# Down products of a two-FFN layer: weight sums on VectorE, and the last layer's outputs of tiles 0 to 3 in a sequence of their own

## The chip, the cores and the metric

The kernel runs on one core of a Trainium2 chip. The metric is the device time of one execution in microseconds (us). Five engines work side by side and meet at semaphores: TensorE (PE; PEld is its weight load), VectorE (DVE), ScalarE (ACT), GpSimd (POOL) and SyncE (SP, which here only issues DMAs). Each engine runs its own instructions strictly in the order in which the program wrote them, so an instruction that waits holds up all that stands behind it on its engine.

## The reference

One layer: a SwiGLU FFN, a token mixer (attention beside a state-space model), a second FFN, a final norm. 1024 tokens, width 1024, FFN width 2816, all float32. The change touches the third matrix product of each FFN, the sums behind it, and the final norm.

```python
def rms_norm(x, g):
    y = x * lax.rsqrt(jnp.mean(x * x, axis=-1, keepdims=True) + EPS)
    return y * g

def swiglu(h, w_gate, w_up, w_down):
    return (jax.nn.silu(h @ w_gate) * (h @ w_up)) @ w_down

x = x + 0.5 * swiglu(rms_norm(x, ffn1_norm), ffn1_w_gate, ffn1_w_up, ffn1_w_down)
...
x = x + 0.5 * swiglu(rms_norm(x, ffn2_norm), ffn2_w_gate, ffn2_w_up, ffn2_w_down)
return rms_norm(x, final_norm)
```

## The kernel before

Each large product is made in float32 precision from three matmuls (`mm3`, L179 to L181): both operands are split into a high part (`hi`, a cast on ACT, L86) and a rest (`lo`, a subtraction on DVE, L87), and the three matmuls are hi*hi, hi*lo and lo*hi. On top of that the product is cut into 2x2 blocks and done with seven block products in place of eight (Strassen's scheme in Winograd's form). This needs sums of blocks of both operands.

**The down product** (`down`, L671) multiplies the FFN's inner activations (in DRAM, `aD`) by `w_down`. `prod(m, ...)` is one of the seven products 0 to 6. It has 11 steps `c`; a step is four row tiles of 128 tokens times three matmuls of 128x512, so 12 matmuls. In the last `tail` steps the order is turned round: for each tile all those steps, then the tile is finished (`fin`).

**Operands.** `next_unit` hands out the operand pairs and makes those of two steps ahead (four units: `wp`, the weights, and `ap`, the activations, in turn). `down_units` (L628) lists them. For products 1 to 4 a unit `wp` has a `pre`: one sum of two weight blocks, 128x512, in place in the loaded weights `wraw` (`tt`, L640) or into a tile `T` (`t1_`, L645). There are 44 such sums in each down product, all on POOL. `pump` issues the `pre` of step c+1 before it makes `ap` of step c. The weights come in with products 0 and 1 (even blocks `ev`, odd blocks `od`); the sums of product 1 need `od`.

**Tiles.** The output is eight tiles of 128 tokens, each in two halves of 512 columns; `X[t]` first holds the residual, and `onto` (L682, DVE) adds a product's result to it. In product 4, `mix0` finishes half 0 of tiles 0 to 3, one tile in each of the first four steps: `onto` from the bank of an earlier product, `before` (the sum of squares on ACT, L204, whose result POOL scales, L206), and `onto` half 1 from a kept sum `U1`. `end0` then finishes half 1 as each tile's tail ends, and calls `after`. Product 5 loads the residual of tiles 4 to 7 (`x1`, step 0) and adds kept sums to them in the four steps from `late` on, which is 4. Product 6 ends tiles 4 to 7 (`end1`).

**The two callers.** In the first FFN `before` and `after` come from `normed`, in the second (and last) they are `gain_first` and `to_out`. `gain_first` also multiplies the half by the norm's gain (L1868, DVE). `to_out` takes the second half's squares, forms the reciprocal root of the mean (`rstd`, nine instructions of 128x1 from L212 to L217, on POOL for tiles 0 to 3 and on DVE for 4 to 7), and queues a function `g` that scales one half on ACT (L1877) and the other on DVE (L1878) and stores each by a DMA from SP (L1880) and from ACT (L1881). `settle(1)` runs the `g` of the tile before, so that it comes one tile late. `run` steps a main generator and its side generators in turn; in the last down product there is no side generator.

Of the kernel before, what the change touches and what calls it, by code (L numbers as in the profile page):

```python
# [18 lines left out]
D = 1024  # L19
# [3 lines left out]
NF = FF // 128  # L23
# [32 lines left out]
def tile_layer(ctx: ExitStack, tc: tile.TileContext, w, out: bass.AP, taps=None):  # L56
    nc = tc.nc
# [22 lines left out]
    def dt_(shape, name):  # L80
        return dram.tile(list(shape), F32, name=name)

    def split(hi, lo, src, scale=None, e=None):

        if scale is None:
            A.copy(out=hi, in_=src)  # L86
            (e or V).tensor_tensor(out=lo, in0=src, in1=hi.bitcast(F32), op=OP.subtract)  # L87
        else:
            A.activation(out=hi, in_=src, func=AF.Copy, scale=scale)
            V.scalar_tensor_tensor(lo, src, scale, hi.bitcast(F32), op0=OP.mult, op1=OP.subtract)  # L90
# [41 lines left out]
    def pair(name):  # L132

        t = slot(name, F32R)
        return t[:, :512], t[:, 512:]
# [47 lines left out]
    HALF = (slice(0, 512), slice(512, 1024))  # L183
# [8 lines left out]
    X, XN, SS = {}, {}, {}  # L192
# [15 lines left out]
    def rstd(t, E):  # L208


        y, r, m, p, z = (SS[t // 4][:, i, t % 4:t % 4 + 1] for i in range(5))
        E.tensor_scalar(y, y, 1.0 / D, p, op0=OP.mult, op1=OP.add)  # L212
        E.tensor_scalar(z, y, -0.5, None, op0=OP.mult)
        E.tensor_scalar(r.bitcast(I32), y.bitcast(I32), -0.5, float(0x5F3759DF), op0=OP.mult, op1=OP.add)
        for _ in range(3):
            E.tensor_scalar(m, r, r, z, op0=OP.mult, op1=OP.mult)
            E.tensor_scalar(r, m, 1.5, r, op0=OP.add, op1=OP.mult)  # L217

    def rstd_one(t, E):

        y, r, m, _, z = (SS[t // 4][:, i, t % 4:t % 4 + 1] for i in range(5))
        E.tensor_scalar(y, y, 1.0 / D, EPS, op0=OP.mult, op1=OP.add)
        E.tensor_scalar(z, y, -0.5, None, op0=OP.mult)
        E.tensor_scalar(r.bitcast(I32), y.bitcast(I32), -0.5, float(0x5F3759DF), op0=OP.mult, op1=OP.add)
        for _ in range(3):
            E.tensor_scalar(m, r, r, z, op0=OP.mult, op1=OP.mult)
            E.tensor_scalar(r, m, 1.5, r, op0=OP.add, op1=OP.mult)

    pend = []

    def settle(left=0):
        while len(pend) > left:
            pend.pop(0)()
# [394 lines left out]
    def down_units(d, n, left):  # L628


        ev, od, t1 = {}, {}, {}

        def load(x, c, r):
            def f():
                x[c] = slot("wraw")
                nc.sync.dma_start(out=x[c], in_=d[128 * r:128 * r + 128, :])
            return f

        def tt(o, a, b, op):
            return lambda: G.tensor_tensor(out=o(), in0=a(), in1=b(), op=op)  # L640

        def t1_(c):
            def f():
                t1[c] = half_slot("T1")
                G.tensor_tensor(out=t1[c], in0=od[c][:, HALF[1]], in1=ev[c][:, HALF[0]], op=OP.subtract)  # L645
            return f

        for m in range(7):
            for c in range(n):
                def e(i, c=c):  # L650
                    return lambda: ev[c][:, HALF[i]]

                def o(i, c=c):
                    return lambda: od[c][:, HALF[i]]

                if m < 2:
                    loads.append(load((ev, od)[m], c, 2 * c + m))
                pre = {1: tt(e(1), o(1), e(1), OP.subtract), 2: tt(e(0), e(1), e(0), OP.add), 3: t1_(c),
                       4: tt(e(0), o(0), e(0), OP.subtract)}.get(m)
                raw = (e(0), o(0), e(0), lambda c=c: t1.pop(c), lambda c=c: od.pop(c)[:, HALF[1]], e(1),  # L660
                       lambda c=c: ev.pop(c)[:, HALF[0]])[m]

                def make(raw=raw):
                    p = pair("wp")
                    split(p[0], p[1], raw())
                    return p

                makes.append((len(loads), pre, make, 9))
                left(m, c)

    def down(n, src, scale, before, after, flag=None, tail=4):  # L671

        U1, U2, U4 = [{} for _ in range(3)]
        pts, late = {}, min(4, n - 1)

        def load_x_(h):
            for t in range(4 * h, 4 * h + 4):
# [85 lines left out]
    def when(flag, gen):  # L763
        while not flag:
            yield
        yield from gen
# [936 lines left out]
    X1, X2 = dt_((8, 128, 1024), "X1"), dt_((8, 128, 1024), "X2")  # L1703

    def run(main, *side, often=()):


        side = list(side)
        for x in main:
            for s in list(side):  # L1710
                if (x != MID or s in often) and next(s, "end") == "end":
                    side.remove(s)
        return side
# [70 lines left out]
    pts = [bank(k) for k in range(KD - 1)]  # L1784
# [4 lines left out]

    squares(0, ALL, 0)  # L1790
    rstd_one(0, V)
    norm_to(0)
    turn_first(0)
    squares(1, ALL, 0)
    rstd_one(1, G)
    for t in (2, 3):
        squares(t, ALL, 0)
# [36 lines left out]
    half0 = []  # L1834
# [22 lines left out]
    half0 = []  # L1857
# [5 lines left out]
    fg = slot("fgain")  # L1863
    A.dma_start(out=fg, in_=w["final_norm"][None, :].to_broadcast([128, D]))

    def gain_first(t, hh):
        squares(t, HALF[hh], 3)
        V.tensor_tensor(out=X[t][:, HALF[hh]], in0=X[t][:, HALF[hh]], in1=fg[:, HALF[hh]], op=OP.mult)  # L1868

    def to_out(t, hh):  # L1870
        squares(t, HALF[hh], 0)
        h, i = divmod(t, 4)
        rstd(t, V if t > 3 else G)

        def g():
            r, o = SS[h][:, 1, i:i + 1], out[0, t * 128:(t + 1) * 128]
            A.activation(out=XN[t][:, HALF[1 - hh]], in_=X[t][:, HALF[1 - hh]], func=AF.Copy, scale=r)  # L1877
            V.scalar_tensor_tensor(XN[t][:, HALF[hh]], X[t][:, HALF[hh]], r, fg[:, HALF[hh]],  # L1878
                                   op0=OP.mult, op1=OP.mult)
            nc.sync.dma_start(out=o[:, HALF[hh]], in_=XN[t][:, HALF[hh]])  # L1880
            A.dma_start(out=o[:, HALF[1 - hh]], in_=XN[t][:, HALF[1 - hh]])  # L1881

        pend.append(g)
        settle(1 if t < 7 else 2)

    drain(run(down(NF // 2, tile_of(X2), 0.5, gain_first, to_out, tail=6)))
    settle()


# [26 lines left out]
```

## Time and profile before

| what | value |
|---|---|
| median of 3 runs | 2109.62 us (2107.64 to 2111.92) |
| the profiled execution | 2110.38 us, span on the core 2108.6 us |
| PE busy in the span | 96%, 9359 matmuls |
| DVE, ACT, POOL busy | 72%, 38%, 21% |
| down product of the first FFN | about 465 to 655 us of the span |
| down product of the second FFN | about 1874 to 2099 us |

The profile is of one execution; its span starts with the first instruction. Rows of the timeline give an instruction's start, its length and, in brackets, how long its engine had been idle before it and what ended that. Rows of the stretches give each engine's busy time and, after an x, the number of instructions that touch the stretch.

### The profile page before, as it was taken

Reading aid. Unit: us, or ns where it says so; the run is one execution under the profiler, and the core shown is the slowest. Engines: PE = TensorE matmul, PEld = TensorE weight load, DVE = VectorE, ACT = ScalarE, POOL = GpSimd, SP = SyncE. Lnnn points to the kernel's source line nnn. Section 1 sums busy time; section 2 is a strip of 40 time slices with the busy share of each in tenths; the row PEclk is TensorE's granted clock in tenths of the full one; section 3 lists DMA queues with packets and bytes.
Section 4 is the critical chain, followed back from the end, with each engine's and each line's share of the span. In section 5 each row is a group of like instructions: output and inputs, shape, how many; then the busy total and the mean of one; then the engine's idle time right before and its main releaser. Section 6 shows DMA issues by size and latency. Waiting matters only on the chain.

```text
span 2108.6 us, 26589 instructions
## 1 busy us (share of the span) xinstructions
PE 2020.0 (96%) x9359; PEld 1618.7 (77%) x9359; DVE 1514.7 (72%) x2684; ACT 802.0 (38%) x1529; POOL 449.1 (21%) x450
## 2 busy tenths in 40 slices
PE   7899999999999899999999999998999999999988
PEld 5687888887868777777777668787788888887866
DVE  7888888678867777877855544625876776769776
ACT  6423323325345422222244652444323233235353
POOL 0121121126441100000000324422121211217350
PEclk9999999999999999999999999999999999999999
DMA  4225324348424143333344556431332233356432
GB/s 160 87 89 169 102 84 132 95 133 321 143 80 157 60 143 98 105 113 107 101 146 140 177 166 205 156 120 51 100 124 92 85 125 100 101 221 228 145 120 80
DMA packets 179561, 272.06 MB, mean 129 GB/s; under 512 B 23576, under 2 KB 110436, under 8 KB 179428
## 3 DMA queue, kind: packets, MB, share of 16 engines
q1 hardware_dynamic: 169008, 264.54, 37.1%
q10 hardware_dynamic: 10308, 5.81, 1.0%
q8 instruction: 74, 1.21, 0.2%
q14 instruction: 59, 0.48, 0.1%
q0 software_dynamic: 112, 0.02, 0.1%
HBM read 191.50 MB, written 81.17 MB: 129 GB/s over the span
## 4 chain that ended last, share of the span: by engine, by line
PE 49%; DVE 10%; DMA 3%; issue 2%; POOL 1%; ACT 1%; SPq 0%; DVEq 0%; ACTq 0%; POOLq 0%
PE bank L179 15%; PE bank L181 14%; PE bank L180 14%; DVE wp L87 2%; PE bank L1239 1%; DMA wraw<-in_ffn_w_down_dram 1%; PE bank L1278 1%; PE bank L1176 1%; PE bank L1263 1%; DVE T L283 1%; DVE ap L87 1%; DVE s L478 1%; PE bank L1174 1%; DVE S L385 1%; DMA al<-Ad 0%
## 5 line engine op out<-in xcount | busy, mean ns | idle before, releaser
L179 PE MATMUL bank<-T,wp 128*128 128x512 f32 x1008 | 399.4, 396 | 8.0 <-DVE F L336 4.2
L181 PE MATMUL bank<-T,wp 128*128 128x512 f32 x1008 | 395.6, 392 | 9.2 <-DVE wp L87 9.2
L180 PE MATMUL bank<-T,wp 128*128 128x512 f32 x1008 | 394.7, 392 | 1.7 <-DVE T L283 1.7
L87 DVE TENSOR_TENSOR wp<-wraw,wp 128x512 fp32r<-128x512 f32 x400 | 326.3, 819 | 82.2 <-ACT wp L86 81.2
L86 ACT CAST wp<-wraw 128x512 fp32r<-128x512 f32 x400 | 244.4, 620 | 294.1 <-DVE wraw L385 162.6
L179 PE MATMUL bank<-b,wp 128*128 128x512 f32 x756 | 304.8, 403 | 17.0 <-DVE s L478 13.6
L181 PE MATMUL bank<-b,wp 128*128 128x512 f32 x756 | 298.8, 395 | 3.5 <-DVE wp L87 3.5
L181 PE MATMUL bank<-wp,ap 128*128 128x512 f32 x744 | 293.7, 395 | 7.4 <-DVE ap L87 6.5
L180 PE MATMUL bank<-b,wp 128*128 128x512 f32 x756 | 298.8, 395 | 0.6 <-DVE b L278 0.6
L180 PE MATMUL bank<-wp,ap 128*128 128x512 f32 x744 | 291.9, 392 | 5.3 <-DVE wp L87 5.3
L179 PE MATMUL bank<-wp,ap 128*128 128x512 f32 x744 | 292.1, 393 | 2.5 <-ACT ap L86 2.5
L181 PEld LDWEIGHTS bank<-T,wp 128*128 128x128 f32 x1008 | 190.3, 189 | 53.2 <-DVE wp L87 13.2
L179 PEld LDWEIGHTS bank<-T,wp 128*128 128x128 f32 x1008 | 190.3, 189 | 51.8 <-issue 10.4
L180 PEld LDWEIGHTS bank<-T,wp 128*128 128x128 f32 x1008 | 190.6, 189 | 41.1 <-DVE T L283 2.9
L87 DVE TENSOR_TENSOR wp<-S,wp 128x512 fp32r<-128x512 f32 x189 | 151.8, 803 | 75.1 <-ACT wp L86 74.6
L86 ACT CAST wp<-S 128x512 fp32r<-128x512 f32 x189 | 116.8, 618 | 223.9 <-DVE S L385 180.4
L599 POOL TENSOR_TENSOR S<-sg 128x512 f32<-128x512 f32 x22 | 33.5, 1523 | 733.2 <-DVE sg L585 449.1
L179 PEld LDWEIGHTS bank<-b,wp 128*128 128x128 f32 x756 | 144.4, 191 | 55.4 <-issue 11.4
L181 PEld LDWEIGHTS bank<-wp,ap 128*128 128x128 f32 x744 | 140.3, 189 | 44.8 <-DVE ap L87 16.3
L181 PEld LDWEIGHTS bank<-b,wp 128*128 128x128 f32 x756 | 144.3, 191 | 36.3 <-DVE wp L87 5.6
L180 PEld LDWEIGHTS bank<-wp,ap 128*128 128x128 f32 x744 | 140.4, 189 | 37.5 <-DVE wp L87 8.6
L180 PEld LDWEIGHTS bank<-b,wp 128*128 128x128 f32 x756 | 144.5, 191 | 29.8 <-DVE b L278 1.2
(247 smaller groups left out, 2820.9 us busy)
## 6 DMA issues: line engine op xcount, KB each, us to landing
araw<-aD SPq DMA_DIRECT2D x154, 256.0 KB
wraw<-in_ffn_w_gate_dram SPq DMA_DIRECT2D x44, 512.0 KB
wraw<-in_ffn_w_up_dram SPq DMA_DIRECT2D x44, 512.0 KB
aD<-sg SPq DMA_DIRECT2D x88, 256.0 KB
wraw<-in_ffn_w_down_dram SPq DMA_DIRECT2D x44, 512.0 KB
wraw<-in_w_in_dram SPq DMA_DIRECT2D x38, 512.0 KB
aD<-S SPq DMA_DIRECT2D x66, 256.0 KB
x<-in_x_dram SPq DMA_DIRECT2D x16, 512.0 KB
```

The costliest lines, as they stand in the source:

```text
L86: A.copy(out=hi, in_=src)
L87: (e or V).tensor_tensor(out=lo, in0=src, in1=hi.bitcast(F32), op=OP.subtract)
L179: P.matmul(pt, lhsT=lhs[0], rhs=rhs[0], start=start, stop=False, skip_group_check=more)
L180: P.matmul(pt, lhsT=lhs[0], rhs=rhs[1], start=False, stop=False, skip_group_check=more)
L181: P.matmul(pt, lhsT=lhs[1], rhs=rhs[0], start=False, stop=stop, skip_group_check=more)
L283: return lambda: V.tensor_tensor(out=p[1], in0=f, in1=p[0].bitcast(F32), op=OP.subtract)
L385: V.tensor_tensor(out=o, in0=c[a], in1=c[b], op=op)
L478: V.tensor_tensor(out=o, in0=pt, in1=t, op=OP.add)
L599: G.tensor_tensor(out=ab[o], in0=ab[a], in1=ab[b], op=op)
L1174: P.matmul(pt, lhsT=KT[:, 2 * q + g2, :], rhs=U[:, 2 * q + g2, :], start=True, stop=False)
L1176: P.matmul(pt[:, 1:128], lhsT=CAv[i][64 * g2:64 * g2 + 64, 128 * q:128 * q + 128], rhs=Vs[64 * g2:64 * g2 + 64, i, q, 0:127], start=False, ...
L1239: P.matmul(pts[j], lhsT=q[64 * j:64 * j + 64, 128 * b:128 * b + 128], rhs=k[64 * j:64 * j + 64, 128 * b + 128 - n:128 * b + 128], start=Tr ...
```

## The change

The sums of weights in the down products of both FFNs are issued on DVE in place of POOL, at the same places of the program. `late` becomes 6, in both FFNs. In the last down product, tiles 0 to 3 no longer take the gain in `gain_first` nor the root and the outputs in `to_out`; a side generator `out_first`, which starts when product 4 has ended, forms one root for the four tiles (`rstd_four`, 12 instructions of 128x4 on DVE) and then, one tile a step, both output halves on DVE with the gain (`gained`) and one DMA of the whole tile from SP. For tiles 4 to 7 `settle()` now runs the `g` of the tile before ahead of this tile's root, and the last tile's outputs are made and stored in quarters of 256 columns.

```diff
+    def rstd_four(h):
+        y, r, m, p, z = (SS[h][:, i] for i in range(5))
+        V.scalar_tensor_tensor(y, y, 1.0 / D, p, op0=OP.mult, op1=OP.add)
+        V.tensor_scalar(z, y, -0.5, None, op0=OP.mult)
+        V.tensor_scalar(r.bitcast(I32), y.bitcast(I32), -0.5, float(0x5F3759DF), op0=OP.mult, op1=OP.add)
+        for _ in range(3):
+            V.tensor_tensor(out=m, in0=r, in1=r, op=OP.mult)
+            V.tensor_tensor(out=m, in0=m, in1=z, op=OP.mult)
+            V.scalar_tensor_tensor(r, m, 1.5, r, op0=OP.add, op1=OP.mult)
...
-            return lambda: G.tensor_tensor(out=o(), in0=a(), in1=b(), op=op)
+            return lambda: V.tensor_tensor(out=o(), in0=a(), in1=b(), op=op)
...
-                G.tensor_tensor(out=t1[c], in0=od[c][:, HALF[1]], in1=ev[c][:, HALF[0]], op=OP.subtract)
+                V.tensor_tensor(out=t1[c], in0=od[c][:, HALF[1]], in1=ev[c][:, HALF[0]], op=OP.subtract)
...
-        pts, late = {}, min(4, n - 1)
+        pts, late = {}, min(6, n - 1)
...
     def gain_first(t, hh):
         squares(t, HALF[hh], 3)
-        V.tensor_tensor(out=X[t][:, HALF[hh]], in0=X[t][:, HALF[hh]], in1=fg[:, HALF[hh]], op=OP.mult)
+        if t > 3:
+            V.tensor_tensor(out=X[t][:, HALF[hh]], in0=X[t][:, HALF[hh]], in1=fg[:, HALF[hh]], op=OP.mult)
+    def gained(t, hh):
+        r = SS[t // 4][:, 1, t % 4:t % 4 + 1]
+        V.scalar_tensor_tensor(XN[t][:, HALF[hh]], X[t][:, HALF[hh]], r, fg[:, HALF[hh]], op0=OP.mult, op1=OP.mult)
+    def out_first():
+        yield
+        rstd_four(0)
+        for t in range(4):
+            yield
+            for hh in range(2):
+                gained(t, hh)
+            nc.sync.dma_start(out=out[0, t * 128:(t + 1) * 128], in_=XN[t])
+            del XN[t], X[t]
     def to_out(t, hh):
         squares(t, HALF[hh], 0)
-        h, i = divmod(t, 4)
-        rstd(t, V if t > 3 else G)
+        if t < 4:
+            return
+        settle()
+        rstd(t, V)
...
+            n, w_ = (2, 256) if t == 7 else (1, 512)
+            for j in range(n):
+                a, b = (slice(512 * x + w_ * j, 512 * x + w_ * j + w_) for x in (1 - hh, hh))
...
         pend.append(g)
-        settle(1 if t < 7 else 2)
+    half0 = []
+    drain(run(down(NF // 2, tile_of(X2), 0.5, gain_first, to_out, half0, tail=6), when(half0, out_first())))
```

Three places in the order of the instructions. First, VectorE at the start of product 4 of the second FFN, before (`wp` and `ap` are the rests of the operands, `x<-bank` and `x<-U` the two `onto`, `x<-x,fgain` the gain):

```order
L87 TENSOR_TENSOR wp<-wraw,wp 128x512
L87 TENSOR_TENSOR ap<-araw,ap 128x512
L682 SCALAR_TENSOR_TENSOR x<-bank_15170,x 128x512
L1868 TENSOR_TENSOR x<-x,fgain 128x512
L682 SCALAR_TENSOR_TENSOR x<-U,x 128x512
L87 TENSOR_TENSOR wp<-wraw,wp 128x512
L87 TENSOR_TENSOR ap<-araw,ap 128x512
```

and in the change:

```order
L87 TENSOR_TENSOR wp<-wraw,wp 128x512
L651 TENSOR_TENSOR wraw<-wraw 128x512
L87 TENSOR_TENSOR ap<-araw,ap 128x512
L693 SCALAR_TENSOR_TENSOR x<-bank_15170,x 128x512
L693 SCALAR_TENSOR_TENSOR x<-U,x 128x512
L87 TENSOR_TENSOR wp<-wraw,wp 128x512
L651 TENSOR_TENSOR wraw<-wraw 128x512
L87 TENSOR_TENSOR ap<-araw,ap 128x512
```

The weight sum stands between the two splits of each step, and the gain is gone. The second place is ScalarE at the end of product 4 of the second FFN, before (casts, squares `xn,ss<-x`, output halves and their DMAs):

```order
L86 CAST ap<-araw 128x512
L204 ACTIVATE xn,ss<-x 128x512 x2
L1877 ACTIVATE xn<-x,ss 128x512
L1881 DMA out_dram<-xn 128x512
L204 ACTIVATE xn,ss<-x 128x512
L1877 ACTIVATE xn<-x,ss 128x512
L1881 DMA out_dram<-xn 128x512
L204 ACTIVATE xn,ss<-x 128x512
L1877 ACTIVATE xn<-x,ss 128x512
L1881 DMA out_dram<-xn 128x512
L86 CAST wp<-wraw 128x512
```

and in the change:

```order
L86 CAST wp<-wraw 128x512
L86 CAST ap<-araw 128x512
L204 ACTIVATE xn,ss<-x 128x512 x4
L86 CAST wp<-wraw 128x512
L86 CAST ap<-araw 128x512
```

Nothing that needs the root stands any more between the squares and the next casts. The third place is VectorE from the end of product 4 to product 5 of the second FFN, before (`x<-bank` is `onto` for half 1 of tiles 2 and 3, `xn<-x,ss,fgain` an output half):

```order
L682 SCALAR_TENSOR_TENSOR x<-bank_15681,x 128x512
L1878 SCALAR_TENSOR_TENSOR xn<-x,ss,fgain 128x512
L682 SCALAR_TENSOR_TENSOR x<-bank_15685,x 128x512
L1878 SCALAR_TENSOR_TENSOR xn<-x,ss,fgain 128x512
L87 TENSOR_TENSOR wp<-wraw,wp 128x512
L87 TENSOR_TENSOR ap<-araw,ap 128x512
```

and in the change:

```order
L693 SCALAR_TENSOR_TENSOR x<-bank_15681,x 128x512
L693 SCALAR_TENSOR_TENSOR x<-bank_15685,x 128x512
L87 TENSOR_TENSOR wp<-wraw,wp 128x512
L87 TENSOR_TENSOR ap<-araw,ap 128x512
L87 TENSOR_TENSOR wp<-wraw,wp 128x512
L87 TENSOR_TENSOR ap<-araw,ap 128x512
L232 SCALAR_TENSOR_TENSOR ss<-ss 128x4
L233 TENSOR_SCALAR ss<-ss 128x4
L234 TENSOR_SCALAR ss<-ss 128x4
L236 TENSOR_TENSOR ss<-ss 128x4
L237 TENSOR_TENSOR ss<-ss 128x4
L238 SCALAR_TENSOR_TENSOR ss<-ss 128x4
```

The last three rows come twice more; then each of the next four steps has its two splits and one tile's two output halves (L1884), and the four steps after these the kept sums of tiles 4 to 7, which before stood two steps earlier.

## Rows read from the trace of the kernel before

**Rows 1.** The page, engines: busy us, share of the span, instructions.

```profile
PE 2020.0 (96%) x9359; PEld 1618.7 (77%) x9359; DVE 1514.7 (72%) x2684; ACT 802.0 (38%) x1529; POOL 449.1 (21%) x450
```

**Rows 2.** Stretches in us: length, busy us (x instructions) by engine, PEclk, DMA share, GB/s.

```profile
515.00:530.00 15.00, 13.54 (x56) 9.82 (x54) 15.00 (x10) 5.21 (x10) 14.05 (x9) 1.00 0.23 70
600.00:617.00 17.00, 14.19 (x51) 8.90 (x51) 16.21 (x19) 8.71 (x17) 7.70 (x6) 1.00 0.00 0
1925.00:1938.00 13.00, 11.63 (x48) 8.36 (x47) 13.00 (x9) 4.55 (x8) 12.32 (x8) 1.00 0.24 67
2006.00:2028.00 22.00, 17.25 (x60) 11.69 (x59) 20.42 (x24) 9.96 (x20) 10.81 (x8) 0.92 0.00 1
2039.00:2048.00 9.00, 6.51 (x21) 4.70 (x20) 6.31 (x11) 6.74 (x14) 7.85 (x13) 0.81 0.77 277
1950.00:1990.00 40.00, 40.00 (x178) 33.14 (x177) 32.70 (x36) 14.93 (x26) 17.81 (x11) 1.00 0.57 184
1888.00:1920.00 32.00, 32.00 (x143) 26.48 (x142) 26.52 (x25) 21.26 (x37) 19.48 (x13) 1.00 1.04 412
```

**Rows 3.** Line 640, weight sums on POOL: ns min/median/max, first and last start us.

```profile
L640 POOL TENSOR_TENSOR wraw<-wraw x66: 1287/1734/1803, 488.5 to 2020.4; 128x512 f32<-128x512 f32 x66
```

**Rows 4.** Groups by line on DVE: count, busy us, mean ns, idle before.

```profile
L385 DVE TENSOR_TENSOR S<-wraw,S 128x512 f32<-128x512 f32 x63 | 57.1, 907 | 0.0
L385 DVE TENSOR_TENSOR S<-wraw 128x512 f32<-128x512 f32 x63 | 43.0, 683 | 0.0
```

**Rows 5.** Timeline of DVE, first FFN, product 4: start, length, instruction, idle before.

```profile
589.59 0.69 DVE L682 SCALAR_TENSOR_TENSOR x<-bank,x 128x512 f32<-128x512 f32 x1
...
593.77 0.68 DVE L682 SCALAR_TENSOR_TENSOR x<-bank,x 128x512 f32<-128x512 f32 x1
594.37 0.68 DVE L682 SCALAR_TENSOR_TENSOR x<-U,x 128x512 f32<-128x512 f32 x1
595.80 1.66 DVE L87 TENSOR_TENSOR wp<-wraw,wp 128x512 fp32r<-128x512 f32 x1 [0.76 <-ACT wp L86]
...
602.20 0.68 DVE L682 SCALAR_TENSOR_TENSOR x<-bank,x 128x512 f32<-128x512 f32 x1
...
613.91 0.68 DVE L87 TENSOR_TENSOR ap<-araw,ap 128x512 fp32r<-128x512 f32 x1
```

**Rows 6.** Timeline of DVE, second FFN, product 4.

```profile
1998.20 0.69 DVE L682 SCALAR_TENSOR_TENSOR x<-bank,x 128x512 f32<-128x512 f32 x1
...
2004.72 0.69 DVE L1868 TENSOR_TENSOR x<-x,fgain 128x512 f32<-128x512 f32 x1 [0.79 <-ACT xn L204]
...
2013.20 0.68 DVE L682 SCALAR_TENSOR_TENSOR x<-bank,x 128x512 f32<-128x512 f32 x1
...
2025.64 0.68 DVE L87 TENSOR_TENSOR ap<-araw,ap 128x512 fp32r<-128x512 f32 x1
```

**Rows 7.** Timeline of ACT, second FFN, start of product 5.

```profile
2040.62 0.72 ACT L1877 ACTIVATE xn<-x,ss 128x512 f32<-128x512 f32 x1 [1.43 <-POOL ss L217]
...
2041.79 0.62 ACT L86 CAST wp<-wraw 128x512 fp32r<-128x512 f32 x1 [0.44 <-ACT xn L1877]
```

**Rows 8.** Timeline of PE: the first matmul after that wait, and the last one.

```profile
2042.98 0.50 PE L179 MATMUL bank<-wp,ap 128*128 128x512 f32 x1 [2.49 <-ACT ap L86]
...
2099.03 0.39 PE L181 MATMUL bank<-wp,ap 128*128 128x512 f32 x1
```

**Rows 9.** Timeline of POOL, second FFN: the first and the eleventh sum of product 1.

```profile
1897.02 1.29 POOL L640 TENSOR_TENSOR wraw<-wraw 128x512 f32<-128x512 f32 x1 [17.93 <-issue]
...
1915.96 20.11 POOL L640 TENSOR_TENSOR wraw<-wraw 128x512 f32<-128x512 f32 x12 [0.28 <-DMA wraw<-in_ffn_w_down_dram]
```

**Rows 10.** Timeline of DVE after the last matmul.

```profile
2100.01 0.68 DVE L682 SCALAR_TENSOR_TENSOR x<-bank,x 128x512 f32<-128x512 f32 x1
2101.56 0.21 DVE L212 TENSOR_SCALAR ss<-ss 128x1 f32<-128x1 f32 x1 [0.86 <-ACT xn L204]
...
2103.61 1.41 DVE L1878 SCALAR_TENSOR_TENSOR xn<-x,ss,fgain 128x512 f32<-128x512 f32 x2
```

**Rows 11.** Timeline of SP's DMA issues, the last two.

```profile
2104.38 0.99 SPq L1880 DMA_DIRECT2D out_dram<-xn  x2
```

More of the change, by code (lines that the diff above doesn't have):

```diff
@@ L1867, in gain_first @@
         squares(t, HALF[hh], 3)
-        V.tensor_tensor(out=X[t][:, HALF[hh]], in0=X[t][:, HALF[hh]], in1=fg[:, HALF[hh]], op=OP.mult)
+        if t > 3:
[12 more added lines that the diff above has]
+            del XN[t], X[t]
     def to_out(t, hh):
         squares(t, HALF[hh], 0)
-        h, i = divmod(t, 4)
-        rstd(t, V if t > 3 else G)
+        if t < 4:
+            return
+        settle()
+        rstd(t, V)
         def g():
[L1876 to L1881, printed above, removed]
+            h, i = divmod(t, 4)
+            o = out[0, t * 128:(t + 1) * 128]
+            n, w_ = (2, 256) if t == 7 else (1, 512)
+            for j in range(n):
+                a, b = (slice(512 * x + w_ * j, 512 * x + w_ * j + w_) for x in (1 - hh, hh))
+                r = SS[h][:, 1, i:i + 1]
+                A.activation(out=XN[t][:, a], in_=X[t][:, a], func=AF.Copy, scale=r)
+                V.scalar_tensor_tensor(XN[t][:, b], X[t][:, b], r, fg[:, b], op0=OP.mult, op1=OP.mult)
+                nc.sync.dma_start(out=o[:, b], in_=XN[t][:, b])
+                A.dma_start(out=o[:, a], in_=XN[t][:, a])
         pend.append(g)
-        settle(1 if t < 7 else 2)
-    drain(run(down(NF // 2, tile_of(X2), 0.5, gain_first, to_out, tail=6)))
+    half0 = []
+    drain(run(down(NF // 2, tile_of(X2), 0.5, gain_first, to_out, half0, tail=6), when(half0, out_first())))
     settle()
```

## The prediction
> **What bounds the kernel now.** I read the page's engine line first: PE is busy 96% of the span [rows 1], so only stretches in which PE stands still, and the end after its last matmul, can give time. Next the stretches. Where PE streams, 178 matmul records touch 40 us [rows 2]. A record is 0.39 us long [rows 8] and starts are 0.227 us apart, so 1.7 of the records only reach over an edge. For any stretch, time lost = length - (records - 1.7) x 0.2268. By this the two down products lose, in [rows 2]:
> - 515 to 530 (first FFN, product 1): 15 - 54.3 x 0.2268 = 2.7 us
> - 600 to 617 (first FFN, product 4): 17 - 49.3 x 0.2268 = 5.8 us
> - 1925 to 1938 (second FFN, product 1): 13 - 46.3 x 0.2268 = 2.5 us
> - 2006 to 2028 (second FFN, product 4): 22 - 58.3 x 0.2268 = 8.8 us
> - 2039 to 2048 (second FFN, product 5): 9 - 19.3 x 0.2268 = 4.6 us
>
> Together 24.4 us. The last two have a granted clock of 0.92 and 0.81 of 2.4 GHz, so a part of each ran at the lower level (1.2 GHz) after PE had stood; that part is in the lost time and goes with the standing.
>
> Then what PE waits for. In 515 to 530, DVE is busy for all 15.00 us with only 10 instructions [rows 2], 1.5 us each, while POOL is busy beside it. Free of POOL, two DVE instructions of this size start 0.60 us apart (593.77 and 594.37, [rows 5]); a split that runs while POOL sums takes 1.66 us (at 595.80, [rows 5]), and the sum takes POOL 1.73 where it takes 1.29 at best [rows 3]. So each slows the other. A step of PE is 12 matmuls, 2.72 us; two slowed splits take more than that, two free ones 1.2. In product 4 a second cause is added: the DVE is idle 0.76 us a step for ACT's cast [rows 5], because the cast stands on ACT behind the squares of the half that DVE has just finished, and in the second FFN 0.79 us more for the gain, which waits for the same squares [rows 6]. In product 5 of the second FFN the chain is another: ACT's output half waits for POOL's root, the casts stand behind it [rows 7], and PE waits 2.49 us for a cast [rows 8].
>
> **The change part by part.**
>
> *Weight sums to DVE.* 44 sums in each down product leave POOL. On DVE each adds one 128x512 instruction with two operands in SBUF. The nearest rows are the same operation on other weights: 0.68 us alone, 0.91 in the mean where POOL disturbs [rows 4]. In a row of such, start to start, it is 0.60 [rows 5]. I take 0.60, since POOL has no large work left there, and keep 0.90 for the range.
>
> Products 1 to 3: a step then costs DVE split, sum, split = 1.8 us against PE's 2.72. A loop limits it too: split 0.60, sum 0.68, ACT's cast of the next weights 0.62 [rows 7], together about 1.92. Both are under 2.72, so the losses of 515 to 530 and 1925 to 1938 go: **2.7 and 2.5 us**. If a sum cost 0.90 the loop would be 2.2, still under.
>
> Product 4: count from the first `onto` of a bank to the end of the rest of step 10's `ap`, which PE waits for. Before, first FFN: 589.59 to 613.91 + 0.68 = 25.0 us [rows 5]. Second FFN: 1998.20 to 2025.64 + 0.68 = 28.1 us [rows 6]. After: from `onto` to the next weight split stays 2.03 us (593.77 to 595.80, [rows 5]), since ACT's squares are still in the chain; then split, sum, split, 1.80, to the next `onto`: 3.83 a step, three steps 11.5. From the fourth `onto`: 2.03, four rounds of the loop at 1.92, then 0.60 + 0.68: 11.0. The first `onto` comes one sum later: 0.6. In all 23.1 us in both FFNs. So the first gains **1.9**, the second **5.0** us (it loses the gain and its wait as well). A step of 3.83 is still longer than 2.72: of the 5.8 and 8.8 us some 3.8 stay in each. With 0.90 a sum, eight sums are on that way, 2.4 us: the first FFN would lose 0.5, the second gain 2.6. If instead the squares dropped out of the chain, all 14.6 would go.
>
> *`late` = 6.* Eight `onto` move two steps later in product 5, to steps 6 to 9: there two splits and two `onto`, 2.4 us of a step of 2.72. It hides under PE; if it did not, 4 x 0.6 us are at stake.
>
> *Outputs of tiles 0 to 3.* The four roots leave POOL and ACT has only the squares there, so casts follow at once: the 2039 to 2048 loss goes, **4.6 us**. What is late next is DVE: `rstd_four` is 12 small instructions; nine of 128x1 take 2.05 us (2101.56 to 2103.61, [rows 10]), so I take 2.7, at most 3.5. It waits for the last squares, and behind it on DVE stand the splits of steps 4 and later of product 5. By my count from product 4's end: `onto` 0.9, squares 0.7, cast 0.6, four splits 2.4, root 3, splits of step 4 1.2: about 9 us, where PE wants them at 4 x 2.72 + 0.45 = 11.3. After that a step has two splits and two output halves, 0.6 x 2 + 0.7 x 2 = 2.6, just under 2.72. So it is hidden, with some 2 us in hand. On SP the four output DMAs wait for DVE, and loads of `araw` stand behind them; those are for at least six steps later (two that are made ahead and four that are loaded beyond them, `rb`), 16 us, so nobody waits. ACT is rid of four output halves.
>
> *The end.* The last matmul starts at 2099.03 [rows 8], its `onto` at 2100.01 [rows 10], about 0.55 us late, since DVE still did the former tile's root and output. With that output put into the 0.86 us wait for the squares [rows 10], DVE is in time: 0.55. Behind the last root two halves took 1.41 us [rows 10]; now two quarters, 0.4 each, and on ACT copy, issue, copy, issue, some 1.5: no gain. The last issue starts at 2105.04 (0.33 before the end of the two, [rows 11]), 3.5 us before the span's end, with 256 KB; now 128 KB; at the 412 GB/s of [rows 2] that is 0.3 less. Sum **0.9 us** (0 to 1.5). The Trainium skill (DMA: Bandwidth & Descriptors, Anatomy of one DMA) speaks against cutting a transfer up: each pays about 2.0 us whatever its size, and bytes at 436 GB/s on top. The 3.5 us behind the last 256 KB agree that most of it is not bytes; whether the fixed parts of two quarters on one queue run side by side, no row shows. If they came one after the other, this term would by the page be a loss of about 1 us, and the sum below 15.7.
>
> **The sum.** 2.7 + 1.9 + 2.5 + 5.0 + 4.6 + 0.9 = 17.6 us. The profiled execution took 2110.38; 2092.8. The median of the runs is 0.8 lower (2109.62): **2092.0 us**. The first FFN's 4.6 must pass through the mixer; PE is its bound too, so I let it pass.
>
> **The rivals.**
> - *DVE becomes the bound.* The sums cost 0.90, the root delays the splits, the end gains 0.3: 2.7 - 0.5 + 2.5 + 2.6 + 4.6 + 0.3 = 12.2, so 2097.4. For: DVE is at 72% [rows 1], and steps of product 4 stay over 2.72. Against: with POOL gone its own instructions get shorter.
> - *The waits of product 4 go altogether.* 24.4 + 1.2 = 25.6, so 2084.0. For: a chain of 3.83 a step for four steps can be covered if DVE starts ahead. Against: DVE waits for PE at the end of product 3 (`keep`), so it starts product 4 with two steps in hand and no more.
> - *The sums wait for the weights on DVE, slower than before.* POOL could wait for `od` with nobody behind it; on DVE the split of step c's `ap` stands behind the sum of step c+1. The blocks arrive 1.89 us apart (1897.02 to 1915.96, ten intervals, [rows 9]) with DMA at 412 GB/s [rows 2]. Product 1 starts 11 steps of 2.72 us after 1874, near 1903.9. Step 9's split is ready at 1897.0 + 10 p + 1.3, and wanted at 1903.9 + 9 x 2.72 + 0.45: at p = 1.89 it is 11 us early; from p = 3.05 PE waits. To eat 17.6 and 4 more in two FFNs, p must be 4.1, that is 190 GB/s. Then about 2114. Nothing new is loaded there.
> - *The gain does not come through.* What PE gains is lost again where a wait of another kind ends at the same time: within 0.2% of before, about 2108.
>
> **How the numbers follow.** My forecast (some waits of product 4 stay) 0.70, with 2088 to 2097 as its own range; DVE as the bound 0.13; all waits gone 0.09; slower 0.04; no gain 0.04. The range reaches from 2086 to 2098, so that it takes in the dear sums and half the way to the case with no waits. 0.2%, 4.2 us, is about what a measurement of this kernel can tell from no change. Faster by more than that 0.92, within it 0.04, slower 0.04.
>
> **What would show it.** In the profile after: weight sums on DVE near 0.68 us each, POOL empty in both down products but for the small instructions; no loss of PE in product 1 of either FFN; in product 4 of both a loss of 3 to 5 us with DVE idle some 0.8 us a step for ACT's cast, and both about equal; no loss of 2 us and more in product 5 of the second FFN; the last `onto` within 0.5 us of the last matmul's start. I am wrong in the main if product 1 still loses time (then POOL was not the cause), or if product 5 shows a new wait for DVE behind the root of four tiles.

## The result, and the profile after

The changed kernel takes **2090.84 us** (median of 4 runs, 2090.54 to 2092.66) against 2109.64 us for the kernel before (4 runs beside it): a ratio of 0.9916, with a 95% interval of 0.9902 to 0.993. That is 18.8 us faster, and the interval leaves out 1. The prediction was 2092.0 us, with a range of 2086 to 2098.

In the profiled execution the span is 2088.8 us. The engine line of the page (busy us, share of the span, instructions), which answers to [rows 1]:

```profile
PE 2012.4 (96%) x9359; PEld 1618.5 (77%) x9359; DVE 1484.3 (71%) x2785; ACT 799.7 (38%) x1526; POOL 290.4 (14%) x326
```

VectorE has 101 instructions more than before and is busy 30 us less. GpSimd has lost 159 us. PE has the same number of matmuls and is busy 7.6 us less. (A matmul that follows a wait is recorded as 0.50 us long, one in a stream as 0.39 [rows 8], so less waiting shortens this figure too.)

The weight sums on VectorE, which answer to [rows 3] (one line's instructions: ns min/median/max, first and last start):

```profile
L651 DVE TENSOR_TENSOR wraw<-wraw x66: 682/684/693, 488.4 to 2009.6; 128x512 f32<-128x512 f32 x66
```

Each of these 66 takes 0.68 to 0.69 us, where POOL took 1.29 to 1.80. The other 22 of the 88, on line 656, take the same. The stretches, which answer to [rows 2] (length, busy us and, after the x, instructions of PE, PEld, DVE, ACT, POOL; granted clock; DMA share; GB/s):

```profile
514.00:529.00 15.00, 15.00 (x67) 12.41 (x67) 13.87 (x23) 8.45 (x15) 0.00 (x0) 1.00 0.34 115
598.00:612.00 14.00, 12.49 (x49) 8.39 (x48) 13.24 (x23) 8.00 (x16) 0.19 (x1) 1.00 0.00 1
1917.00:1930.00 13.00, 13.00 (x59) 10.77 (x58) 11.41 (x19) 6.85 (x12) 0.00 (x0) 1.00 0.39 119
1999.00:2015.00 16.00, 14.51 (x58) 10.16 (x58) 14.59 (x25) 9.26 (x20) 0.39 (x2) 1.00 0.12 35
2030.00:2042.00 12.00, 12.00 (x55) 9.93 (x54) 12.00 (x20) 5.55 (x11) 0.00 (x0) 1.00 0.87 299
```

With the formula of the prediction, lost = length - (records - 1.7) x 0.2268, the terms read as follows:

| place | lost before | lost after | gained | forecast |
|---|---|---|---|---|
| first FFN, product 1 | 2.7 | 0.2 (no wait) | 2.5 | 2.7 |
| first FFN, product 4 | 5.8 | 14 - 47.3 x 0.2268 = 3.3 | 2.5 | 1.9 |
| second FFN, product 1 | 2.5 | 0 | 2.5 | 2.5 |
| second FFN, product 4 | 8.8 | 16 - 56.3 x 0.2268 = 3.2 | 5.6 | 5.0 |
| second FFN, product 5 | 4.6 | 0 | 4.6 | 4.6 |
| last matmul's start to the span's end | 9.54 | 8.51 | 1.03 | 0.9 |
| sum | | | 18.7 | 17.6 |

(For the last row the last matmuls start at 2099.03 and 2080.26, and the spans to the hundredth are 2108.56 and 2088.77 us; the differences are taken before rounding.) The loss of product 4 is the one that stays. VectorE there, in the first FFN, which answers to [rows 5] (start, length, instruction, and in brackets how long VectorE had been idle and what ended that):

```profile
593.46 0.69 DVE L87 TENSOR_TENSOR wp<-wraw,wp 128x512 fp32r<-128x512 f32 x1 [0.76 <-ACT wp L86]
594.07 0.68 DVE L651 TENSOR_TENSOR wraw<-wraw 128x512 f32<-128x512 f32 x1
594.67 0.69 DVE L87 TENSOR_TENSOR ap<-araw,ap 128x512 fp32r<-128x512 f32 x1
595.27 0.68 DVE L693 SCALAR_TENSOR_TENSOR x<-bank,x 128x512 f32<-128x512 f32 x1
595.87 0.68 DVE L693 SCALAR_TENSOR_TENSOR x<-U,x 128x512 f32<-128x512 f32 x1
597.32 0.69 DVE L87 TENSOR_TENSOR wp<-wraw,wp 128x512 fp32r<-128x512 f32 x1 [0.76 <-ACT wp L86]
...
602.99 0.69 DVE L87 TENSOR_TENSOR wp<-wraw,wp 128x512 fp32r<-128x512 f32 x1
603.59 0.69 DVE L651 TENSOR_TENSOR wraw<-wraw 128x512 f32<-128x512 f32 x1
604.19 0.69 DVE L87 TENSOR_TENSOR ap<-araw,ap 128x512 fp32r<-128x512 f32 x1
604.79 0.69 DVE L87 TENSOR_TENSOR wp<-wraw,wp 128x512 fp32r<-128x512 f32 x1
```

A step goes from 593.46 to 597.32, 3.86 us, while PE needs 2.72: four starts 0.60 apart, then the 0.69 of the last `onto` and 0.76 idle for ACT's cast. After the four steps with `onto` a step is 1.80 us without any idle time (602.99 to 604.79), and VectorE catches up.

At the end, VectorE after the last matmul (which starts at 2080.26), answering to [rows 10]:

```profile
2080.69 0.69 DVE L693 SCALAR_TENSOR_TENSOR x<-bank,x 128x512 f32<-128x512 f32 x1 [0.39 <-PE bank L181]
2081.30 0.74 DVE L1912 SCALAR_TENSOR_TENSOR xn<-x,ss,fgain 128x512 f32<-128x512 f32 x1
2082.24 0.21 DVE L212 TENSOR_SCALAR ss<-ss 128x1 f32<-128x1 f32 x1 [0.20 <-ACT xn L204]
...
2084.41 0.88 DVE L1912 SCALAR_TENSOR_TENSOR xn<-x,ss,fgain 128x256 f32<-128x256 f32 x2
```

Now VectorE is idle until PE has the bank: the last `onto` starts 0.43 us after the last matmul's start, where it was 0.98 before. The output of tile 6 (2081.30) fills the wait for ACT's squares.

### The profile page after: what moved, and what is told of

Its sections match the earlier page's. It is cut to its first block, busy times and chain, and to the rows that moved or that the text cites. A ratio compares the mean times of both kernels' runs of the same rounds, so it can differ in the third digit from the quotient of the medians.

```text
span 2088.8 us, 26458 instructions
## 1 busy us (share of the span) xinstructions
PE 2012.4 (96%) x9359; PEld 1618.5 (77%) x9359; DVE 1484.3 (71%) x2785; ACT 799.7 (38%) x1526; POOL 290.4 (14%) x326
## 4 chain that ended last, share of the span: by engine, by line
PE 53%; DVE 8%; ACT 1%; issue 1%; DMA 1%; POOL 1%; SPq 0%; DVEq 0%; ACTq 0%; POOLq 0%
PE bank L179 16%; PE bank L181 16%; PE bank L180 16%; DVE wp L87 1%; PE bank L1250 1%; PE bank L1289 1%; PE bank L1187 1%; PE bank L1274 1%; DVE T L294 1%; DVE s L489 1%; PE bank L1185 1%; DMA uo<-Od 1%; DVE S L396 0%; DMA al<-Ad 0%; DVE Vs L1148 0%
## 5 line engine op out<-in xcount | busy, mean ns | idle before, releaser
L87 DVE TENSOR_TENSOR wp<-wraw,wp 128x512 fp32r<-128x512 f32 x400 | 291.8, 732 | 90.7 <-ACT wp L86 88.8
L181 PEld LDWEIGHTS bank<-wp,ap 128*128 128x128 f32 x744 | 139.6, 188 | 37.5 <-DVE ap L87 9.0
L180 PEld LDWEIGHTS bank<-wp,ap 128*128 128x128 f32 x744 | 139.7, 188 | 31.5 <-DVE wp L87 2.8
L179 PEld LDWEIGHTS bank<-wp,ap 128*128 128x128 f32 x744 | 139.7, 188 | 28.9 <-ACT ap L86 0.7
```

The source lines that it names most:

```text
L179: P.matmul(pt, lhsT=lhs[0], rhs=rhs[0], start=start, stop=False, skip_group_check=more)
L180: P.matmul(pt, lhsT=lhs[0], rhs=rhs[1], start=False, stop=False, skip_group_check=more)
L181: P.matmul(pt, lhsT=lhs[1], rhs=rhs[0], start=False, stop=stop, skip_group_check=more)
```

## The experiments

All ratios are against the kernel before, run on the same chip at the same time; its median was 2108.63 us beside the first four kernels, 2108.43 beside the next four and 2109.88 beside the last three. The theory was the prediction's: the sums on POOL slow VectorE's splits and are slowed by them (product 1); in product 4 ACT's squares hold the casts; in product 5 the root on POOL does; and the three don't touch each other. The rivals were that it is not POOL's reading that slows VectorE but something else that left with the sums; that one half of the change alone gives it all; and, for the end, that quarters cost more than they bring.

**The sums alone.** The kernel before with the sums on VectorE:

```diff
-            return lambda: G.tensor_tensor(out=o(), in0=a(), in1=b(), op=op)
+            return lambda: V.tensor_tensor(out=o(), in0=a(), in1=b(), op=op)
...
-                G.tensor_tensor(out=t1[c], in0=od[c][:, HALF[1]], in1=ev[c][:, HALF[0]], op=OP.subtract)
+                V.tensor_tensor(out=t1[c], in0=od[c][:, HALF[1]], in1=ev[c][:, HALF[0]], op=OP.subtract)
```

> The kernel before with the weight sums on DVE, and nothing else of the change. My theory (POOL and DVE slow each other): the losses of product 1 go in both FFNs (2.7 and 2.5 us), product 4 of the first FFN loses 3.2 in place of 5.8, product 4 of the second still has the gain and its wait, about 4.5 us a step in place of 5.0, and loses about 6 in place of 8.8; product 5 of the second FFN keeps its 4.6, the end is as before. In all 10.6 us faster, near 2099. Rival (the time came from the output sequence and the missing gain, the sums hardly count): at most 4 us faster.

2098.98 us (6 runs), ratio 0.9955 (0.994 to 0.9971). Its stretches, columns as above:

```profile
515.00:530.00 15.00, 15.00 (x68) 12.41 (x67) 13.98 (x23) 8.00 (x14) 0.00 (x0) 1.00 0.29 93
598.00:612.00 14.00, 12.46 (x49) 8.43 (x48) 13.23 (x23) 8.01 (x16) 0.19 (x1) 1.00 0.00 1
1995.00:2014.00 19.00, 15.71 (x59) 10.24 (x58) 17.36 (x30) 9.76 (x20) 1.39 (x2) 1.00 0.01 2
2025.00:2036.00 11.00, 8.49 (x29) 6.29 (x28) 8.14 (x14) 6.91 (x14) 8.59 (x14) 0.84 0.81 300
```

Product 1 loses nothing, product 4 of the first FFN 3.3 us as with the whole change. Product 4 of the second FFN loses 19 - 57.3 x 0.2268 = 6.0, because the gain and its wait are still there; product 5 still loses 11 - 27.3 x 0.2268 = 4.8 behind POOL's root.

**The outputs alone.** The change with both sums back on POOL:

```diff
-            return lambda: V.tensor_tensor(out=o(), in0=a(), in1=b(), op=op)
+            return lambda: G.tensor_tensor(out=o(), in0=a(), in1=b(), op=op)
...
-                V.tensor_tensor(out=t1[c], in0=od[c][:, HALF[1]], in1=ev[c][:, HALF[0]], op=OP.subtract)
+                G.tensor_tensor(out=t1[c], in0=od[c][:, HALF[1]], in1=ev[c][:, HALF[0]], op=OP.subtract)
```

> The whole change but for the sums, which stay on POOL. My theory: the product 1 losses stay (2.7 and 2.5), product 4 of the first FFN stays at 5.8, product 4 of the second comes down to the first's 5.8 from 8.8 (no gain and no wait for it), the product 5 loss of 4.6 goes, the end gives 1.0: about 8.6 us faster than before, near 2101, and with the run of the sums alone the two gains add up to the whole 18.8. Rival (the parts hide each other): the two add up to over 23 or under 14.

2100.37 us (5 runs), ratio 0.996 (0.9945 to 0.9974). Its stretches:

```profile
517.00:528.00 11.00, 9.68 (x39) 6.71 (x37) 11.00 (x8) 4.17 (x8) 10.45 (x7) 1.00 0.28 72
2006.00:2024.00 18.00, 15.36 (x58) 10.28 (x58) 15.50 (x19) 9.75 (x20) 6.57 (x5) 1.00 0.10 30
2036.00:2046.00 10.00, 10.00 (x46) 8.29 (x45) 10.00 (x17) 5.06 (x10) 0.00 (x0) 1.00 0.82 282
```

Product 1 loses 2.5 us, as before the change, with VectorE busy throughout on eight instructions. Product 5 loses nothing. Product 4 of the second FFN loses 5.2: the outputs' part alone gives 3.6 of the 5.6 us there, and the sums alone 2.8 (8.8 - 6.0), so that the two overlap there by 0.8. Together the two halves gain 9.65 + 8.26 = 17.9 us; the whole change gained 18.4 in the runs beside the last three kernels and 18.8 in its first ones. They add up, within what the intervals can tell; neither alone explains the result.

**Is it POOL's reading?** Two kernels put useless work back on POOL, the sums staying on VectorE; nothing reads what it writes. In the first, two additions of 128x256 read each sum again:

```diff
+                for j in (0, 256):
+                    G.tensor_tensor(out=junk(), in0=o()[:, j:j + 256], in1=o()[:, j:j + 256], op=OP.add)
```

> The changed kernel with extra work on POOL that nobody needs: after each weight sum on DVE, POOL adds its result to itself in two halves of 128x256 and writes them to a tile that is not read. No result depends on it, so POOL is in no chain. My theory (the loss of product 1 came from POOL and DVE slowing each other): DVE's splits beside it take 1.2 to 1.8 us again, PE loses 2 us and more in product 1 of both FFNs and more in product 4, in all 5 to 18 us slower than the changed kernel, 2096 to 2109. Rival (the loss came from waiting for POOL's results): within 1.5 us of the changed kernel, 2091.

2102.19 us (8 runs), ratio 0.9976 (0.9966 to 0.9986). The second reads one column of the sum, so as to start at the same time, and then only fills, four times 128x256:

```diff
+                G.tensor_scalar(junk()[:, :1], o()[:, :1], 1.0, None, op0=OP.mult)
+                for j in range(4):
+                    G.memset(junk(), 0.0)
```

> The changed kernel with other extra work on POOL that nobody needs: after each weight sum, one tiny read of its result (128x1, so that POOL keeps pace) and four fills of a 128x256 tile with zeros, which read nothing. Theory A (a POOL instruction slows a split on DVE only where it reads SBUF): DVE's splits stay near 0.68 us, within 1.5 us of the changed kernel, 2090 to 2092.5. Theory B (any work on POOL slows DVE): splits of over 1 us beside the fills, product 4 loses time as with the extra reads, 2096 and more.

2089.39 us (4 runs), ratio 0.9908 (0.9891 to 0.9925): no different from the change. VectorE and POOL in the reading kernel, product 1 of the first FFN (timelines):

```profile
506.28 1.10 DVE L87 TENSOR_TENSOR wp<-wraw,wp 128x512 fp32r<-128x512 f32 x1
507.30 1.10 DVE L656 TENSOR_TENSOR wraw<-wraw 128x512 f32<-128x512 f32 x1
508.32 0.68 DVE L87 TENSOR_TENSOR ap<-araw,ap 128x512 fp32r<-128x512 f32 x1
508.92 1.10 DVE L87 TENSOR_TENSOR wp<-wraw,wp 128x512 fp32r<-128x512 f32 x1
```

```profile
505.89 1.96 POOL L658 TENSOR_TENSOR junk<-wraw 128x256 f32<-128x256 f32 x2 [0.68 <-POOL junk L658]
```

and the groups of the filling kernel over 500 to 530 us (count, busy us and mean ns of one, idle time):

```profile
L659 POOL MEMSET junk<- 128x256 f32 x62 | 19.4, 313 | 3.6
...
L87 DVE TENSOR_TENSOR wp<-wraw,wp 128x512 fp32r<-128x512 f32 x16 | 11.0, 691 | 1.1
L87 DVE TENSOR_TENSOR ap<-araw,ap 128x512 fp32r<-128x512 f32 x16 | 11.0, 687 | 0.2 <-ACT ap L86 0.2
...
L657 POOL TENSOR_SCALAR junk<-wraw 128x1 f32<-128x1 f32 x16 | 5.7, 355 | 1.6 <-POOL junk L659 0.3
```

POOL is busy some 25 of these 30 us, 19.4 of them with filling, and VectorE's splits keep 0.69 us. In the reading kernel each POOL addition reads half as much as a weight sum did. Two of them stand in a step, and two of VectorE's three instructions in it take 1.10 in place of 0.68. So the slowing comes with POOL's reading additions, and not with POOL being busy or writing. The Trainium skill (SBUF — State Buffer, Who interferes with whom) says the same: a VectorE instruction with two inputs in SBUF contends with a GpSimd instruction that reads SBUF, not with one that only writes it. Whether a POOL instruction with one large operand slows VectorE as well, no run here shows.

One part of the expectation missed: I expected the reading kernel to lose time in product 1. It does not, since a step there is 506.28 to 508.92, 2.64 us, still under PE's 2.72. Its loss comes from product 4 instead. The stretch of the first FFN:

```profile
598.00:622.00 24.00, 19.30 (x70) 13.34 (x69) 19.41 (x27) 10.30 (x22) 13.18 (x24) 0.93 0.11 44
```

24 - 68.3 x 0.2268 = 8.5 us lost, against 3.3 in the same stretch of the change: VectorE, late after the four steps with `onto`, catches up with steps of 2.65 (splits of `wp` at 604.03 and 606.68) in place of 1.80, and so hardly at all.

**Are the squares the cause in product 4?** The change, with each tile's squares one step later, ahead of that step's `onto` in the program:

```diff
+            if 0 < c < 5:
+                before(c - 1, 0)
...
-                before(c, 0)
```

> The changed kernel, but in product 4 the squares of half 0 of a tile are issued one step later, so that ACT's casts no longer stand behind squares that wait for DVE. My theory (what is left of product 4's loss is this chain of onto, squares, cast, split at 3.86 us a step): DVE takes 3.0 us a step in place of 3.86 and the idle time for ACT's cast goes; product 4 loses under 0.7 us in each FFN in place of 3.2 and 3.1, so about 5 us faster than the changed kernel, near 2086. Rival (DVE's own work is the bound in product 4): the loss stays above 2.5 us in each and the time within 1 us of the changed kernel.

2084.48 us (4 runs), ratio 0.9891 (0.9875 to 0.9908). Its stretches at product 4 of the two FFNs, and VectorE there:

```profile
595.00:611.00 16.00, 16.00 (x72) 13.20 (x71) 13.49 (x23) 8.42 (x18) 2.07 (x8) 1.00 0.15 63
1995.00:2012.00 17.00, 17.00 (x77) 14.01 (x76) 14.97 (x25) 9.61 (x21) 0.71 (x2) 1.00 0.10 33
```

```profile
589.66 0.68 DVE L693 SCALAR_TENSOR_TENSOR x<-U,x 128x512 f32<-128x512 f32 x1
590.26 0.68 DVE L87 TENSOR_TENSOR wp<-wraw,wp 128x512 fp32r<-128x512 f32 x1
...
593.27 0.68 DVE L87 TENSOR_TENSOR wp<-wraw,wp 128x512 fp32r<-128x512 f32 x1
```

The idle 0.76 is gone, a step is 590.26 to 593.27, 3.01 us, and PE doesn't stop: 16 - 70.3 x 0.2268 and 17 - 75.3 x 0.2268 are both 0 within 0.1. VectorE is still 0.3 us a step over PE's 2.72, but for four steps only, and what PE has in hand covers that. Both FFNs' product 4 together lost 6.5 in the change.

To compare on one chip, the change and this kernel were run again, beside a third one.

> The changed kernel again, on the same chip as the next two, as their measure. 2090 to 2092, 0.991 to 0.992 of before.

> The kernel with the squares one step later again, beside the changed kernel on one chip. Theory (the chain over ACT's squares is the rest of product 4's loss, 6.3 us in both FFNs): 5.5 to 6.5 us faster than the changed kernel. Rival (a part of it is given back): under 4 us.

The change: 2091.44 us (5 runs), ratio 0.992 (0.9906 to 0.9933). With the squares a step later: 2084.73 us (4 runs), ratio 0.9882 (0.9869 to 0.9896). The difference is 6.7 us, near the 6.5 of the two stretches.

**The quarters, and `late`.** The change with halves for the last tile, and the change with `late` at 4:

```diff
-            n, w_ = (2, 256) if t == 7 else (1, 512)
+            n, w_ = 1, 512
```

> The changed kernel, but the last tile is made and stored in halves of 512 columns, not in quarters. My theory (a smaller last transfer is 0.3 us shorter and nothing else changes): 0.3 us slower than the changed kernel, from the last matmul to the end 8.8 in place of 8.5 us. Rival 1 (two quarters on a queue pay their fixed part one after the other): 1 us and more faster. Rival 2 (four issues cost what the smaller transfer saves): no difference, within 0.2 us at the end.

```diff
-        pts, late = {}, min(6, n - 1)
+        pts, late = {}, min(4, n - 1)
```

> The changed kernel with late = 4 again, in both FFNs, so that the kept sums of tiles 4 to 7 are added in steps 4 to 7 of product 5, two of which also hold outputs of tiles 2 and 3 in the second FFN. My theory (the move by two steps hides under PE, and DVE has some 2 us in hand behind the root): no loss in the first FFN, at most 0.5 us in product 5 of the second, within 1 us of the changed kernel. Rival (the move is needed): steps 4 and 5 hold 3.7 us of DVE work, DVE falls 2 us behind and PE loses 1 to 2 us there.

With halves 2091.95 us (5 runs), ratio 0.9919 (0.9904 to 0.9933); with `late` 4, 2091.8 (4 runs), ratio 0.9915 (0.9898 to 0.9932). Neither can be told from the change by its time. For the end the trace tells more. ACT's last instructions, first with halves (span 2090.2, last matmul at 2081.33), then with quarters (span 2088.8, last matmul at 2080.26):

```profile
2085.49 0.72 ACT L1911 ACTIVATE xn<-x,ss 128x512 f32<-128x512 f32 x1 [1.67 <-DVE ss L217]
2086.24 0.37 ACTq L1914 DMA_DIRECT2D out_dram<-xn  x1
```

```profile
2084.41 0.51 ACT L1911 ACTIVATE xn<-x,ss 128x256 f32<-128x256 f32 x1 [1.67 <-DVE ss L217]
2084.95 0.37 ACTq L1914 DMA_DIRECT2D out_dram<-xn  x1
2085.37 0.51 ACT L1911 ACTIVATE xn<-x,ss 128x256 f32<-128x256 f32 x1 [0.44 <-ACT xn L1911]
2085.90 0.34 ACTq L1914 DMA_DIRECT2D out_dram<-xn  x1
```

From the last matmul's start to the span's end (2090.18 to the hundredth) it is 8.85 us with halves and 8.51 with quarters, 0.34 less. That is one execution with halves; the ten profiled ones with quarters, of all kernels, lie between 8.50 and 8.52. The last issue comes later in quarters (5.64 after the last matmul against 4.91), but the end follows it 2.9 us later in place of 3.9. From the first of the two issues to the end it is 3.8 us for two quarters, no more than the 3.9 for one half. So the fixed part of a store is not paid twice in a row: the two run side by side here. `late` is not needed: the losses of PE are the same at 4 and at 6, none in product 5 of the second FFN.

**What is left in the first FFN.** After the squares are put off, the profile shows two waits of PE in the first FFN, 1.3 us for a split that stands behind POOL's roots and 1.1 for the norm at the transposes (waits of PE from 575 to 660 us: line, waited for, sum, times, longest):

```profile
PE bank L180 <- DVE wp L87: 1.3, 1, 1.3
PE bank L273 <- DVE xn L248: 1.1, 1, 1.1
```

The first try only put the norms of tiles 0 to 3 off until four had gathered, with the roots still on POOL:

```diff
-            settle(1)
+            settle(lag if t < 4 else 1)
...
-    drain(run(down(NF // 2, tile_of(xin), 0.5, *normed(X1), half0),
+    drain(run(down(NF // 2, tile_of(xin), 0.5, *normed(X1, lag=4), half0),
```

> The kernel with the squares one step later, and in the first FFN the norms of tiles 0 to 3 put off until after product 5's steps, so that DVE does not wait for POOL's roots ahead of the splits of product 5. My theory (PE's 1.9 us loss at the start of product 5 of the first FFN is DVE waiting for POOL's roots): that loss goes, 1.9 us faster than with the later squares alone, near 2082.5. Rival (the loss is given back later, at the transposes that read the norms): no more than 0.5 us faster than with the later squares alone.

2086.91 us (5 runs), ratio 0.9894 (0.9878 to 0.991): no gain over the squares put off alone (0.9891 and 0.9882 in its two measurements). The first wait is gone, but four norms now stand in a row in front of the transposes, and PE waits for each. Its waits from 575 to 660 us, and the stretch behind them, first in this kernel, then with the squares put off alone:

```profile
PE bank L273 <- DVE xn L248: 2.3, 4, 1.4
```

```profile
647.00:655.00 8.00, 8.00 (x31) 6.68 (x32) 2.81 (x5) 5.47 (x11) 0.30 (x1) 0.65 0.01 2
647.00:655.00 8.00, 6.88 (x40) 5.66 (x39) 4.97 (x8) 5.87 (x12) 0.30 (x1) 1.00 0.01 2
```

That theory fell: the wait was moved and not removed. After the four waits the granted clock is 0.65, so that PE ran a part of this stretch at its lower level (1.2 GHz). The hundred matmuls around the transposes, up to the one that starts at 653.50 us, take 27.1 us here and 22.5 with the squares put off alone, so more is lost there than the first wait had cost. The second try gives the first FFN what the change gave the second: one root for four tiles on VectorE in product 5, and then one tile's norm a step.

```diff
+            if later_root and t < 4:
+                nc.sync.dma_start(out=keep[t], in_=X[t])
+                return
...
+    def norm_first():
+        yield
+        rstd_four(0)
+        for t in range(4):
+            yield
+            norm_to(t)
+            del X[t]
...
-    drain(run(down(NF // 2, tile_of(xin), 0.5, *normed(X1), half0),
+    drain(run(down(NF // 2, tile_of(xin), 0.5, *normed(X1, later_root=True), half0), when(half0, norm_first()),
```

> The kernel with the squares one step later, and in the first FFN one root for tiles 0 to 3 on DVE in step 1 of product 5 and their norms in steps 2 to 5, so that no split of product 5 stands behind a wait for POOL's roots, and the norms are ready before the transposes. Theory (the 1.9 us at the start of product 5 are the wait for POOL, and putting the norms off lost time only because they then came together, right ahead of the transposes): that loss goes without a new one, 1.5 to 2 us faster than with the later squares alone. Rival (the first FFN's end has another bound): no more than 0.5 us faster.

**2082.19 us** (4 runs), ratio 0.9868 (0.9855 to 0.9882): 2.5 us under the kernel with the squares put off (2084.73), 9.2 under the change on the same chip, and the fastest of all. The stretch in which the first wait was, with the squares put off alone and then here:

```profile
612.00:630.00 18.00, 16.63 (x72) 13.17 (x71) 10.08 (x16) 7.24 (x16) 14.46 (x32) 1.00 0.72 271
612.00:630.00 18.00, 18.00 (x81) 14.88 (x81) 11.86 (x28) 8.15 (x19) 0.00 (x0) 1.00 0.87 321
```

18 - 70.3 x 0.2268 = 2.1 us lost, and now 18 - 79.3 x 0.2268 = 0. The view of PE's waits lists none between 575 and 660 us: the wait at the transposes, which the expected 1.5 to 2 us did not count, is gone as well.

## Why the prediction was right, point by point

**Sums on VectorE.** A sum was taken at 0.60 from start to start; it is (594.07 to 594.67). In products 1 to 4 POOL has nothing left but single small instructions, product 1 loses nothing in either FFN, and the loss comes back when the sums go back to POOL. That POOL's reading additions slow VectorE, and not a wait for their results or a busy POOL, is shown by the reading and the filling kernel.

**Product 4.** The step was forecast at 3.83 and measured at 3.86, with the 0.76 for the cast. The mis-sized term is the loop behind it: split, sum and cast were put at 1.92 a round, and a round takes 1.80, VectorE without idle time; the cast is not on that way. Four rounds make some 0.5 us in each FFN, and this is most of the 0.6 by which both product 4 terms were too small. That the squares hold the casts was argued from the order, and is shown by putting them off: the loss goes to nothing in both FFNs.

**`late`.** It costs nothing, as forecast. It brings nothing either: with 4 the time is the same within the intervals, and so are PE's losses.

**Outputs of tiles 0 to 3.** Product 5 of the second FFN loses nothing. The root of four takes VectorE 2.1 us in place of the 2.7 taken, and no wait stands behind it:

```profile
2025.26 0.15 DVE L232 SCALAR_TENSOR_TENSOR ss<-ss 128x4 f32<-128x4 f32 x1
...
2027.38 0.69 DVE L87 TENSOR_TENSOR wp<-wraw,wp 128x512 fp32r<-128x512 f32 x1
...
2031.11 1.41 DVE L1884 SCALAR_TENSOR_TENSOR xn<-x,ss,fgain 128x512 f32<-128x512 f32 x2
...
2033.65 1.41 DVE L1884 SCALAR_TENSOR_TENSOR xn<-x,ss,fgain 128x512 f32<-128x512 f32 x2
```

A step with two output halves is 2.54 us (2.6 forecast), just under PE's 2.72.

**The end.** 1.03 in place of 0.9. The last `onto` gave the 0.55 that was forecast, the quarters 0.34 for 0.3. The remaining 0.14, which the kernel with halves has too, was put at nothing. By the order of the instructions it goes with VectorE's output half of tile 6, which before stood between the last root and the half of tile 7 ([rows 10]) and now stands ahead of that root. That the quarters' number came out is in part luck. The forecast had the last issue at the same place and 0.3 less behind it; against the kernel with halves the issue is 0.73 later and there is 1.07 less behind it. The prediction's rival at this place, that two quarters pay one after the other the fixed part of about 2.0 us (the Trainium skill, DMA: Bandwidth & Descriptors, Anatomy of one DMA), does not hold here: the kernel with halves is the longer one. That section is on DMAs that GpSimd issues, and these are issued by SyncE and ScalarE, so no run here measures its 2.0 us.

**The rivals.** VectorE did not become the bound: its sums cost 0.60, not 0.90. The waits of product 4 did not all go: 3.3 and 3.2 us of PE's time stayed, and taking them away gives the 2084 that this rival named, by a change in another place. The sums did not wait for weights in a way that PE sees (1917 to 1930 loses nothing; of the 66 sums on line 651 two found VectorE idle for weights, 1.0 us in all). No new wait ate the gain.

**What the terms leave over.** The terms of the first FFN explain 5.0 us, but the second down product starts 6.12 us earlier (1867.56 against 1873.68 for its first matmul). In the second profile of the change (the run beside the last two kernels) it starts at 1868.01, 5.7 us earlier. So 0.7 to 1.1 us are gained between the two FFNs, where nothing was changed, and two executions of the same kernel differ there by 0.45 us. That is no more than scatter. From the matmul that starts at 660.63 us before, behind the first FFN, to the first one of the second down product, none of the kernels was changed; this takes 1213.05 us before, 1211.88 and 1212.51 in the two profiles of the change, and 1208.5 to 1213.9 over all thirteen profiled executions. The granted clock differs there (from 1307 to 1325 us it is 1.00 in the first profile of the change and 0.91 in the second). The terms and the 1.1 of the first profile make the 19.8 us by which the profiled span is shorter; the medians differ by 18.8.

## What to carry to other kernels

Where PE waits for VectorE and GpSimd is busy, compare one VectorE instruction beside GpSimd's reads with the same one alone: here the work took less time on the already busier engine, because each engine had been slowing the other. An instruction that is in nobody's hurry (squares for a norm) belongs behind the operands that PE wants next on its engine, and a root that several tiles need can be formed once for all. A norm or a root that is put off has to be spread out again before its reader, or the wait only moves.

## What the runs showed of the hardware

- A VectorE addition or subtraction of 128x512 with both operands in SBUF takes 0.68 us alone and 1.10 beside a POOL addition that reads 128x256; POOL's two additions took 1.96. Two of them in a step lengthen two of VectorE's three instructions: the split at 508.32 keeps its 0.68, though POOL's next addition starts at 508.53, before it has ended.
- POOL filling 128x256 (0.31 us each, 62 in 30 us) leaves VectorE at 0.69.
- A chain of twelve small instructions over 128x4 took VectorE 2.1 us, hardly more than nine over 128x1 (2.05, [rows 10]).
- Two stores of 128 KB issued 0.95 us apart from one queue ended earlier after the last matmul (8.51 us) than one of 256 KB (8.85), although the second was issued later than that one (5.64 us after the last matmul against 4.91).
- After PE had waited four times for a norm, 2.3 us in all, its granted clock was 0.65 over the next 8 us; after a single wait of 1.1 us it stayed at 1.00.
